# Another share of the taps of a 31-tap convolution for GpSimd, with its products formed on ScalarE, and the attention mask loaded a stage earlier

## The chip, the cores and the metric

The kernel runs on one core of a Trainium2 chip. The metric is the device time of one execution in microseconds, here as the median of several runs; one more execution was recorded by the hardware profiler, and every row below is from that one. PE is TensorE (its weight loads are PEld), DVE is VectorE, ACT is ScalarE, POOL is GpSimd and SP is SyncE, which only issues transfers here.

## The reference

The reference is a two-layer diffusion backbone over 1024 latent tokens and 256 context tokens with a model width of 1024. The change is in the token mixer of the first layer, which has two parallel parts: a convolution module on 512 channels and an attention of 8 heads inside a window. Cut to what matters:

```python
def conformer_conv(z, conv_w, conv_b, ln_g, ln_b):
    val, gate = z[..., :512], z[..., 512:]
    u = val * jax.nn.sigmoid(gate)
    u = dwconv(u, conv_w, conv_b, 15, 15)        # 31 taps, each channel by itself
    return jax.nn.silu(layer_norm(u, ln_g, ln_b))

def mixer_ab(hl, hc, w_in, ...):
    glu, q, k, v = split(h @ w_in)               # for latent and context tokens
    a = conformer_conv(glu, ...)
    b = window_gqa_latent(rope(q), q, rope(k), v, k_ctx, v_ctx, sink)
    return concat(a, b) @ w_out

# inside the attention, for blocks of 128 queries:
s_lat = where(abs(qpos - kpos) <= 128, q @ k.T * scale, -1e30)
p_lat, p_ctx, _ = joint_softmax([s_lat, s_ctx, sink])
```

## The kernel before

The tokens lie in the free dimension and the channels on the 128 partitions. They come in three groups of 512, 512 and 256 (`TOK`). Every projection is done with weights and activations split into a high and a low part, three matmuls for each slice of 128 input channels (lines 316 to 318). `wcol` loads a block of 128 output columns on SP's queue (line 291), ScalarE rounds it to the high part `wh` (line 296), and line 299 subtracts to get the low part `wl`, on VectorE or GpSimd as the letters of `WS` for the stage say in turn.

`proj0` is the stage of the projections of layer 0. Its steps stand in `PROJ0`: `glu(i)` makes the gated input U of one of four blocks of 128 convolution channels, from two weight blocks; `qproj` and `kvproj` make q, k and v. `gemm` takes PSUM from a pool of four banks (`mm`). After each `gemm`, `pump` advances background generators by a time that it is credited with: the convolutions (`conv`), the modulation vectors (`mods`), and the stacking of the queries (`qstack`).

`conv(i, U)` does one block of channels. The accumulator A lies in the three PSUM banks of the pool `ca`, of which there is one. ScalarE starts it with the middle tap (line 642). Of the other 30 taps, VectorE adds 22 into A, one instruction of 1295 columns each (line 654). The first 8 (`PTAPS`) go to GpSimd: one instruction forms a product P (line 649) in one of two buffers `cp`, and another adds it to the one before (line 651). Line 657 adds both sums on VectorE into `co`, from where three transfers on SP's queue (line 659) store it to HBM. The layer norm reads it from there in the course of the attention.

`mods(0, 1..3, None, pa)` runs in the background of this stage with its tiles in the stage's pool. Its matmul results leave PSUM through line 346, on ScalarE.

`attn0` follows. It closes `ca`, opens the two double banks `big` for the scores in its place, and opens the SBUF pool `m0b` where `m0a`, the pool of `proj0`, has been. Its first act is to load the mask `msk` (1152 columns) and the sinks on ScalarE's queue (lines 805 and 807). For each pair of heads and block of queries, `scores` computes scores into `big` (lines 865 and 872), adds the mask and takes the maximum on VectorE (line 877), exponentiates on ScalarE (line 882) and divides; `pv` transposes and multiplies by v. 40 such steps are chained, three of them ahead of their `pv`.

The order of the instructions on each engine is fixed at build time by a planner. It goes by the order of the program and by its own estimate of when an instruction can start, so a later instruction may be put ahead of an earlier one on the same engine. On the chip each engine then works through its list in order. A tile that lies where an earlier tile has been waits until that one's readers have ended, transfers too.

Of the kernel before, what the change touches and what calls it, by code (L numbers as in the profile page):

```python
# [11 lines left out]
F32 = mybir.dt.float32  # L12
F32R = mybir.dt.float32r
AF = mybir.ActivationFunctionType
ALU = mybir.AluOpType
# [5 lines left out]
SEQ = 1024  # L21
CTX = 256
# [3 lines left out]
TOK = (512, 512, 256)  # L26
# [6 lines left out]
LAGC = 2  # L33
GRPS = 3, 3, 3, 3, 3, 3, 1, 3
SQB = 3
P0W = "V"
YR = 6.0
YP = 18.0
YL = 1.5, 1.0, 1.5
# [2 lines left out]
YF = 6.0  # L42
O0 = "G"
MS = ((0, 5), (1, 1), (1, 0), (1, 2), (1, 4), (1, 3), (1, 5)), ()
PTAPS = 8
WS = {"p0": P0W, "o0": O0, "f0": "GV", "c0": "GV", "p1": "GV", "m1": "G", "o1": "V", "f1": "G"}
PB0 = 4
LAG0 = 3
# [51 lines left out]
def tile_backbone(ctx: ExitStack, tc: tile.TileContext, a: dict, out: bass.AP):  # L100
    nc = tc.nc
    V, S, G, T = nc.vector, nc.scalar, nc.gpsimd, nc.tensor
# [21 lines left out]
    def nm(s):  # L124
        uid[0] += 1
        return f"{s}{uid[0]}"
# [17 lines left out]
    def page(shape, dt=F32, s="pg"):  # L144
        return pgp.tile(shape, dt, tag="pg", name=nm(s))
# [59 lines left out]
    def tmp(n=512, dt=F32):  # L205
        return tp.tile([128, 512], dt, tag="t512", name=nm("t"), bufs=4)[:, 0:n]
# [55 lines left out]
    for r, items in enumerate(rows):  # L262
        n = 0
# [71 lines left out]
    def mods(l, idx, pre=None, pool=None):  # L335
        w = 512 if pre else (256 if pool else 128)

        def load(n, q):
            raw = (pool or wmp[0]).tile([128, 4, w], F32, tag="wm", name=nm("wm"), bufs=2)
            c0 = idx * D + n * w  # L340
            nc.sync.dma_start(raw, a["w_mod"][l, q * 512:q * 512 + 512, c0:c0 + w].rearrange("(k p) m -> p k m", p=128))
            return raw

        def fin(ps, n):
            t = tmp(w)
            (S.copy if pool else V.tensor_copy)(t, ps)
            yield YF
            pr = bank()
            nb = w // 128
            for m in range(nb):  # L350
                T.matmul(pr[:, 2 * m:2 * m + 2], t[:, m * 128:m * 128 + 128], sel, start=True, stop=True)
            mod_fin(l, idx, nb * n, nb, 2, pr)

        if pre:
            pss = [bank(), bank()]
            for q in range(2):
                for n in range(2):
                    for j in range(4):
                        T.matmul(pss[n][32 * j:32 * j + 32], sc[:, q * 4 + j], pre[q * 4 + j][:, n * 512:n * 512 + 512], start=q == 0, stop=q == 1)
            for n in range(2):  # L360
                yield from fin(pss[n], n)
            return
        nn = 1024 // w
        raws = [load(0, 0), load(0, 1)]
        yield 6.0
        for n in range(nn):
            ps = bank()[:, 0:w]
            for q in range(2):
                for j in range(4):
                    T.matmul(ps[32 * j:32 * j + 32], sc[:, q * 4 + j], raws[q][:, j], start=q == 0, stop=q == 1)  # L370
                if n + 1 < nn:
                    raws[q] = load(n + 1, q)
            yield from fin(ps, n)
            yield YM0 if pool else YM
# [235 lines left out]
    CW, UW = SEQ + 15 + CTX, SEQ + 15 + CTX + 30  # L610
    COFF = (0, 512, SEQ + 15)

    def mixer0(hs, nxt, xs0):
        w = a["ab_w_in"][0]
        pc = ph[0]
        rcos, rsin = pc.tile([128, 1024], F32, name="rcos", bufs=1), pc.tile([128, 1024], F32, name="rsin", bufs=1)
        protr = pc.tile([128, 3, 128], F32R, name="protr", bufs=1)
        with tc.tile_pool(name="m0a", bufs=1) as pa:
            prep = proj0(hs, w, pa, rcos, rsin, protr, xs0)
        psum_side("big", 2)  # L620
        cat = Lazy()
        with tc.tile_pool(name="m0b", bufs=1) as pb:
            attn0(pb, *prep, cat)
        ws[0] = "o0"
        with tc.tile_pool(name="m0o", bufs=8 * len(YPO)) as po:
            for i, g in enumerate(GO0):
                if i < 2:
                    spawn(cat.load(GO0[i + 1]), "cat")
                ys, sq, last = outproj(a["ab_w_out"][0], cat, g, (lambda g: [po.tile([128, 512], F32, tag="y", name=nm("y")) for _ in range(8)]) if g in YPO else (lambda g: acts(g, 8, F32, "y")), lambda g: PO0[g], range(7, -1, -1) if g in OR0 else None)
                drain("cat")  # L630
                spawn(update(0, g, ys, sq, 2, last, True, (0, 3, 4) if g < 2 else None, nxt, PU0[g]))
            pumping[0] = True
            while not posted >= {(0, g) for g in YPO}:
                advance(flows["norm"])
            pumping[0] = False

    def proj0(hs, w, pa, rcos, rsin, protr, xs0):
        def conv(i, U):
            wc = lambda k: cols("acw", k * 4 + i)
            A = wide()[:, 0:CW]  # L640
            B = None
            S.activation(A, U[:, 15:15 + CW], AF.Identity, scale=wc(15), bias=cols("acb", i))
            taps = [k for k in range(31) if k != 15]
            pt, dt = taps[:PTAPS], taps[PTAPS:]
            nch = 6
            for c in range(nch):
                for k in pt[c::nch]:
                    P = pa.tile([128, CW], F32, tag="cp", name=nm("cp"), bufs=2)
                    G.tensor_scalar(P, U[:, k:k + CW], wc(k), 1.0, ALU.mult, ALU.mult)
                    if B is not None:  # L650
                        G.tensor_add(P, P, B)
                    B = P
                for k in dt[c::nch]:
                    V.scalar_tensor_tensor(A, U[:, k:k + CW], wc(k), A, ALU.mult, ALU.add)
                yield CY
            O = pa.tile([128, CW], F32, tag="co", name=nm("co"), bufs=2)
            V.tensor_add(O, A, B)
            for g in range(3):
                nc.sync.dma_start(cd[g][:, i], O[:, COFF[g]:COFF[g] + TOK[g]])

        st = pa.tile([128, CW], F32, tag="cp", name=nm("par"), bufs=2)
        for r in range(1, 5):
            spawn(params(r, st[:, r * 128 - 128:r * 128]), "par")

# [29 lines left out]
        def kvproj():  # L694
            prot = tmp(384).rearrange("p (a b) -> p a b", a=3)
            nc.scalar.dma_start(prot, a["rot"])
            V.tensor_copy(protr, prot)
            wk, wv = wcol(w, 1536), wcol(w, 1664)
            for g in range(3):
                n = TOK[g]  # L700
                ps = bank()[:, 0:n]
                gemm(ps, wk, *hs[g])
                if g < 2:
                    kh, kl = tmp(dt=F32R), tmp(dt=F32R)
                    split(ps, kh, kl)
                else:
                    V.tensor_copy(KFC[:, 0], ps)
                p2 = bank()[:, 0:n]
                gemm(p2, wv, *hs[g])
                S.copy(VF[:, OFF[g]:OFF[g] + n] if g < 2 else KFC[:, 1], p2)  # L710
                if g < 2:
                    pp = bank()
                    T.matmul(pp, protr[:, 0], kh, start=True, stop=False)
                    T.matmul(pp, protr[:, 0], kl, start=False, stop=True)
                    dst, m2 = KF[:, OFF[g]:OFF[g] + n], tmp()
                    V.tensor_mul(dst, ps, rcos[:, OFF[g]:OFF[g] + n])
                    V.tensor_mul(m2, pp, rsin[:, OFF[g]:OFF[g] + n])
                    V.tensor_add(dst, dst, m2)
# [81 lines left out]
        drain("bg")  # L800
        return KH[0:2], KH[2], vstack, kstack, qstack, qs

    def attn0(pc, KH, KC, vstack, kstack, qstack, qs, cat):
        msk = pc.tile([128, 1152], F32, name="msk")
        nc.scalar.dma_start(msk, a["win_mask"])
        sink = pc.tile([128, 8], F32, name="sink")
        nc.scalar.dma_start(sink, a["b_sink"].to_broadcast([128, 8]))
        nsink = pc.tile([128, 8], F32, name="nsink")
        V.tensor_scalar_mul(nsink, sink, -1.0)

        cath, catl = [[], [], []], [[], [], []]

# [38 lines left out]
        def scores(i, b, RAW, ROT, res):  # L851
# [6 lines left out]
            for j in range(2):  # L858
                s = bank2()
                if b < 8:  # L860
                    k0, k1 = max(0, b - 1), min(8, b + 2)
                    nw = 128 * (k1 - k0)
                    kt = list(range(k0, k1)) + [8, 9]
                    for x in range(2):
                        T.matmul(s[:, 512 - nw:512], ROT[j][:, b * 128:b * 128 + 128], KH[kv][x][:, k0 * 128:k1 * 128], start=x == 0, stop=x == 1)
                    q = RAW[j][0][:, b * 128:b * 128 + 128]
                    mk = msk[:, 0:640] if 0 < b < 7 else (msk[:, 128:640] if b == 0 else msk[:, 640:1152])
                else:
                    nw, kt, mk = 0, [8, 9], msk[:, 384:640]
                    q = RAW[j][1][:, (b - 8) * 128:(b - 8) * 128 + 128]  # L870
# [960 lines left out]
```

## Time and profile before

| | us |
|---|---|
| median of 3 runs | 3089.76 (3085.82 to 3090.44) |
| the profiled execution, its own time | 3090.51 |
| its span, first to last instruction | 3088.7 |
| PE busy in the span | 2934.9 (95%) |
| DVE busy | 1746.5 (57%) |
| ACT busy | 1093.5 (35%) |
| POOL busy | 991.6 (32%) |

The time outside the span is 1.8 us. PE's busy time counts overlapping matmuls by modelled ends, so what tells is where PE stands idle and at which granted clock it works: 1.00 is 2.4 GHz and 0.50 is 1.2 GHz.

### The profile page before, as it was taken

Reading aid. Unit: us, or ns where it says so; the run is one execution under the profiler, and the core shown is the slowest. Engines: PE = TensorE matmul, PEld = TensorE weight load, DVE = VectorE, ACT = ScalarE, POOL = GpSimd, SP = SyncE. Lnnn points to the kernel's source line nnn. Section 1 sums busy time; section 2 is a strip of 40 time slices with the busy share of each in tenths; the row PEclk is TensorE's granted clock in tenths of the full one; section 3 lists DMA queues with packets and bytes.
Section 4 is the critical chain, followed back from the end, with each engine's and each line's share of the span. In section 5 each row is a group of like instructions: output and inputs, shape, how many; then the busy total and the mean of one; then the engine's idle time right before and its main releaser. Section 6 shows DMA issues by size and latency. Waiting matters only on the chain. (4 is left out here: it accounts for less than half of the span.)

```text
span 3088.7 us, 37477 instructions
## 1 busy us (share of the span) xinstructions
PE 2934.9 (95%) x14441; PEld 2351.5 (76%) x14441; DVE 1746.5 (57%) x2631; ACT 1093.5 (35%) x1631; POOL 991.6 (32%) x730
## 2 busy tenths in 40 slices
PE   6997899899999999999999789999998999999998
PEld 4886777678888888889987556666686888888886
DVE  4799883664654555558645886667355132232234
ACT  4213784532221122145533763333344322111213
POOL 4676445821110011055432351110253222112223
PEclk8998999999999999999999899999999999999999
DMA  8343113434432444269844230010152121111212
GB/s 296 117 132 99 38 34 109 139 104 132 143 128 78 130 140 144 84 195 280 275 148 145 92 112 27 31 39 28 58 160 89 48 62 55 34 44 53 62 41 109
DMA packets 330768, 327.04 MB, mean 106 GB/s; under 512 B 27121, under 2 KB 280734, under 8 KB 330590
## 3 DMA queue, kind: packets, MB, share of 16 engines
q1 hardware_dynamic: 326784, 321.74, 32.5%
q10 hardware_dynamic: 3806, 2.91, 0.3%
q8 instruction: 113, 1.85, 0.2%
q14 instruction: 65, 0.53, 0.1%
HBM read 255.36 MB, written 69.21 MB: 105 GB/s over the span
## 5 line engine op out<-in xcount | busy, mean ns | idle before, releaser
L299 POOL TENSOR_TENSOR wl<-wr,wh 128x1024 fp32r<-128x1024 f32 x154 | 380.7, 2472 | 1302.6 <-ACT wh L296 1253.6
L296 ACT CAST wh<-wr 128x1024 fp32r<-128x1024 f32 x248 | 259.7, 1048 | 1063.1 <-PE big L317 678.8
L316 PE MATMUL big<-hh,wh 128*128 128x512 f32 x1376 | 540.4, 393 | 4.9 <-DVE ga L1489 2.7
L317 PE MATMUL big<-hl,wh 128*128 128x512 f32 x1376 | 537.9, 392 | 3.1 <-POOL hl L504 3.1
L318 PE MATMUL big<-hh,wl 128*128 128x512 f32 x1376 | 537.5, 391 | 0.6 <-DVE wl L299 0.6
L316 PE MATMUL mm<-hh,wh 128*128 128x256 f32 (+1 forms) x1000 | 346.3, 347 | 10.8 <-DVE i L1035 9.5
L317 PE MATMUL mm<-hl,wh 128*128 128x256 f32 (+1 forms) x1000 | 339.0, 339 | 4.5 <-POOL hl L504 2.6
L318 PE MATMUL mm<-hh,wl 128*128 128x256 f32 (+1 forms) x1000 | 337.8, 338 | 3.3 <-POOL wl L299 2.3
L316 PEld LDWEIGHTS big<-hh,wh 128*128 128x128 f32 x1376 | 260.1, 189 | 61.5 <-ACT hh L499 3.4
L317 PEld LDWEIGHTS big<-hl,wh 128*128 128x128 f32 x1376 | 260.1, 189 | 58.7 <-POOL hl L504 4.3
L318 PEld LDWEIGHTS big<-hh,wl 128*128 128x128 f32 x1376 | 259.9, 189 | 55.4 <-DVE wl L299 1.0
L1557 PE MATMUL mm<-zh,wh 128*128 128x512 f32 x704 | 276.6, 393 | 1.2 <-ACT xt L1660 0.7
L1559 PE MATMUL mm<-zh,wl 128*128 128x512 f32 x704 | 275.4, 391 | 0.0
L1558 PE MATMUL mm<-zl,wh 128*128 128x512 f32 x704 | 274.9, 391 | 0.3 <-DVE zl L323 0.3
L1564 DVE TENSOR_TENSOR acc<-acc,mm 128x512 f32<-128x512 f32 x224 | 150.7, 685 | 179.5 <-PE mm L1559 179.2
L474 POOL TENSOR_TENSOR sq<-t,sq 128x512 f32<-128x512 f32 (+1 forms) x153 | 194.6, 1274 | 170.5 <-ACT t L470 153.9
L1489 DVE SCALAR_TENSOR_TENSOR ga<-big,C,ga 128x1023 f32<-128x1023 f32 x86 | 110.2, 1281 | 235.1 <-ACT ga L1502 233.7
L316 PEld LDWEIGHTS mm<-hh,wh 128*128 128x128 f32 x1000 | 192.3, 192 | 37.3 <-DVE i L1035 9.9
L317 PEld LDWEIGHTS mm<-hl,wh 128*128 128x128 f32 x1000 | 192.1, 192 | 30.1 <-POOL hl L504 5.4
L318 PEld LDWEIGHTS mm<-hh,wl 128*128 128x128 f32 x1000 | 191.9, 192 | 24.2 <-POOL wl L299 3.2
L399 DVE SCALAR_TENSOR_TENSOR wa<-wm,sc,wa 128x256 f32<-128x256 f32 x280 | 149.2, 558 | 89.8 <-DMA wm<-in_w_mod_dram 87.5
L299 DVE TENSOR_TENSOR wl<-wr,wh 128x1024 fp32r<-128x1024 f32 x94 | 131.6, 1400 | 108.4 <-ACT wh L296 104.4
(350 smaller groups left out, 5267.7 us busy)
## 6 DMA issues: line engine op xcount, KB each, us to landing
wr<-in_ffn_w_up_dram SPq DMA_DIRECT2D x132, 512.0 KB, 4.9
wm<-in_w_mod_dram SPq DMA_DIRECT2D x224, 128.0 KB, 2.2
wr<-in_ffn_w_down_dram SPq DMA_DIRECT2D x44, 512.0 KB, 3.5
wm<-in_w_mod_dram SPq DMA_DIRECT2D x40, 512.0 KB, 7.4
xd<-x SPq DMA_DIRECT2D x38, 512.0 KB, 4.4
x<-xd SPq DMA_DIRECT2D x38, 512.0 KB, 5.8
wr<-in_ab_w_out_dram SPq DMA_DIRECT2D x24, 512.0 KB, 7.5
wdd<-wh SPq DMA_DIRECT2D x22, 512.0 KB, 2.6
```

What stands on the lines that cost most here:

```text
L296: S.copy(hi[:, 0:nk, 0:m], raw[:, 0:nk, 0:m])
L299: (G if e[wn[0] % len(e)] == "G" else V).tensor_sub(lo[:, 0:nk, 0:m], raw[:, 0:nk, 0:m], f32(hi[:, 0:nk, 0:m]))
L316: T.matmul(ps, wh, xh[k], start=i == 0, stop=False)
L317: T.matmul(ps, wh, xl[k], start=False, stop=False)
L318: T.matmul(ps, wl, xh[k], start=False, stop=i == n - 1)
L399: V.scalar_tensor_tensor(acc[:, v], raw, sc[:, k, v:v + 1], acc[:, v], ALU.mult, ALU.add)
L474: self.eng.tensor_add(self.acc[-1], t, self.acc[-1])
L1489: V.scalar_tensor_tensor(dst[:, lo:hi], src[:, lo + d - o:hi + d - o], k, dst[:, lo:hi], ALU.mult, ALU.add)
L1557: T.matmul(ps, wh, zh, start=j == j0, stop=False)
L1558: T.matmul(ps, wh, zl, start=False, stop=False)
L1559: T.matmul(ps, wl, zh, start=False, stop=j == j1 - 1)
L1564: V.tensor_add(ys[g][c], ys[g][c], ps)
```

## The change

GpSimd's part of a convolution grows from 8 taps to 10, and VectorE's shrinks from 22 to 20. The products for GpSimd are formed by ScalarE, in three buffers in place of two, so that GpSimd only adds. The stage's weight splits alternate between GpSimd and VectorE (`P0W`), where all were on VectorE. The results of `mods` leave PSUM on VectorE. The last convolution's result goes to a page of the kernel's common pool (`page`, 24 of 4 KB per partition) and a common temporary tile, as two additions, where it went to the stage's pool as one. Mask and sinks get a place in the mixer's outer pool and are loaded in `kvproj`, on ScalarE's queue; the part of the mask that only the last block needs is loaded as before, in `attn0`.

```diff
-P0W = "V"
+P0W = "VG"
-PTAPS = 8
+PTAPS = 10
 WS = {"p0": P0W, "o0": O0, ...}
...
         def fin(ps, n):
             t = tmp(w)
-            (S.copy if pool else V.tensor_copy)(t, ps)
+            V.tensor_copy(t, ps)
...
         with tc.tile_pool(name="m0a", bufs=1) as pa:
-            prep = proj0(hs, w, pa, rcos, rsin, protr, xs0)
+            masks = [pc.tile([128, n], F32, name=s_, bufs=1) for s_, n in (("msk", 640), ("sink", 8), ("nsink", 8))]
+            prep = proj0(hs, w, pa, rcos, rsin, protr, xs0, masks)
...
                 for k in pt[c::nch]:
-                    P = pa.tile([128, CW], F32, tag="cp", name=nm("cp"), bufs=2)
-                    G.tensor_scalar(P, U[:, k:k + CW], wc(k), 1.0, ALU.mult, ALU.mult)
+                    P = pa.tile([128, CW], F32, tag="cp", name=nm("cp"), bufs=3)
+                    S.mul(P, U[:, k:k + CW], wc(k))
                     if B is not None:
                         G.tensor_add(P, P, B)
                     B = P
...
-            O = pa.tile([128, CW], F32, tag="co", name=nm("co"), bufs=2)
-            V.tensor_add(O, A, B)
+            if i < 3:
+                O = pa.tile([128, CW], F32, tag="co", name=nm("co"), bufs=1)
+                V.tensor_add(O, A, B)
+                parts = [O[:, COFF[g]:COFF[g] + TOK[g]] for g in range(3)]
+            else:
+
+                O, OC = page([128, 1024], F32, "co"), tmp(CTX)
+                V.tensor_add(O, A[:, 0:SEQ], B[:, 0:SEQ])
+                V.tensor_add(OC, A[:, SEQ + 15:CW], B[:, SEQ + 15:CW])
+                parts = [O[:, 0:512], O[:, 512:1024], OC]
             for g in range(3):
-                nc.sync.dma_start(cd[g][:, i], O[:, COFF[g]:COFF[g] + TOK[g]])
+                nc.sync.dma_start(cd[g][:, i], parts[g])
...
         def kvproj():
             prot = tmp(384).rearrange("p (a b) -> p a b", a=3)
             nc.scalar.dma_start(prot, a["rot"])
+            nc.scalar.dma_start(masks[0], a["win_mask"][:, 0:640])
+            nc.scalar.dma_start(masks[1], a["b_sink"].to_broadcast([128, 8]))
+            V.tensor_scalar_mul(masks[2], masks[1], -1.0)
             V.tensor_copy(protr, prot)
...
-        msk = pc.tile([128, 1152], F32, name="msk")
-        nc.scalar.dma_start(msk, a["win_mask"])
-        sink = pc.tile([128, 8], F32, name="sink")
-        nc.scalar.dma_start(sink, a["b_sink"].to_broadcast([128, 8]))
-        nsink = pc.tile([128, 8], F32, name="nsink")
-        V.tensor_scalar_mul(nsink, sink, -1.0)
+        msk, sink, nsink = masks
+        msk7 = pc.tile([128, 512], F32, name="msk7")
+        nc.scalar.dma_start(msk7, a["win_mask"][:, 640:1152])
```

## Rows read from the trace of the kernel before

**Rows 1.** Stretches of 50 us: busy time (instructions) per engine, granted clock, DMA share, GB/s.

```profile
150.00:200.00 50.00, 50.00 (x294) 40.88 (x293) 47.92 (x37) 8.98 (x14) 37.53 (x20) 1.00 0.53 160
300.00:350.00 50.00, 37.47 (x293) 30.59 (x294) 43.46 (x109) 33.76 (x70) 19.74 (x28) 0.79 0.26 80
400.00:450.00 50.00, 48.71 (x446) 38.74 (x444) 41.79 (x115) 42.76 (x91) 29.15 (x40) 1.00 0.01 2
```

**Rows 2.** Waits of PE, 60 to 302 us and 302 to 460 us: total, times, longest.

```profile
PE mm L755 <- POOL sraw L751: 3.0, 1, 3.0
...
PE big L865 <- DVE mx L877: 11.2, 6, 8.9
PE big L865 <- DVE co L657: 7.0, 1, 7.0
```

**Rows 3.** Timeline of the change of stage: start, duration, instruction, idle before.

```profile
295.15 0.44 PE L735 MATMUL mm<-ident,kfc 128*128 128x128 f32 x2 [0.56 <-ACT t L784]
301.06 1.50 DVE L657 TENSOR_TENSOR co<-ca,cp 128x1295 f32<-128x1295 f32 x1
302.58 1.28 SPq L659 DMA_DIRECT2D cd<-co  x3
302.61 0.79 PE L865 MATMUL big<-k,srot 128*128 128x256 f32 x2 [7.03 <-DVE co L657]
307.10 2.84 DVE L751 TENSOR_TENSOR sraw<-qsrc,sraw 64x512 fp32r<-64x512 f32 x4
307.40 0.35 ACTq L805 DMA_DIRECT2D msk<-in_win_mask_dram  x1
312.36 0.98 POOL L220 TENSOR_SCALAR p<-sink 128x2 f32<-128x2 f32 x4 [12.73 <-DMA qsrc<-qd]
312.88 0.68 DVE L877 CUSTOM_DVE_ANT_0 p<-big,msk 128x512 f32<-128x512 f32 x1
313.63 1.01 PE L865 MATMUL big<-k,srot 128*128 128x384 f32 x2 [8.94 <-DVE mx L877]
```

**Rows 4.** Stretches of 10 us around both idle times, columns as in rows 1.

```profile
270.00:280.00 10.00, 6.34 (x24) 4.53 (x23) 9.96 (x5) 0.00 (x0) 9.77 (x5) 0.84 0.32 103
280.00:290.00 10.00, 10.00 (x50) 8.60 (x49) 9.81 (x12) 1.41 (x3) 3.28 (x4) 0.82 0.21 65
310.00:320.00 10.00, 5.83 (x19) 5.46 (x20) 7.85 (x23) 4.52 (x9) 1.68 (x5) 0.50 0.37 118
```

**Rows 5.** DVE's groups, 60 to 302 us: count | busy, mean ns of one | idle before.

```profile
L654 DVE SCALAR_TENSOR_TENSOR ca<-u,C,ca 128x1295 f32<-128x1295 f32 x88 | 138.0, 1568 | 4.7 <-ACT ca L642 2.9
L299 DVE TENSOR_TENSOR wl<-wr,wh 128x1024 fp32r<-128x1024 f32 x11 | 22.5, 2047 | 3.6 <-ACT wh L296 3.6
L657 DVE TENSOR_TENSOR co<-ca,cp 128x1295 f32<-128x1295 f32 x4 | 6.0, 1501 | 0.9 <-POOL cp L651 0.9
L707 DVE COPY kfc<-mm 128x256 f32<-128x256 f32 x1 | 0.4, 408 | 0.0
```

**Rows 6.** POOL's groups, 60 to 302 us.

```profile
L651 POOL TENSOR_TENSOR cp<-cp,cp 128x1295 f32<-128x1295 f32 x28 | 86.8, 3100 | 2.3
L649 POOL TENSOR_SCALAR cp<-u,C 128x1295 f32<-128x1295 f32 x32 | 47.4, 1480 | 39.5 <-DVE co L657 14.6 <-DVE u L687 12.7 <-PE mm L275 9.5
L299 POOL TENSOR_TENSOR wl<-wr,wh 128x1024 fp32r<-128x1024 f32 x3 | 8.0, 2692 | 6.9 <-PE mm L735 6.9
```

**Rows 7.** ACT's groups: the first 60 to 302 us, the second 302.5 to 460 us.

```profile
L642 ACT ACTIVATE ca<-u,C 128x1295 f32<-128x1295 f32 x4 | 5.7, 1434 | 6.0 <-DVE co L657 6.0
...
L224 ACT ACTIVATE p<-p,den 128x640 f32<-128x640 f32 x24 | 19.9, 828 | 2.0 <-DVE den L884 1.6
```

**Rows 8.** Timeline of ACT, POOL and DVE at single places.

```profile
55.34 1.23 DVE L299 TENSOR_TENSOR wl<-wr,wh 128x1024 fp32r<-128x1024 f32 x1
157.65 0.60 ACT L679 ACTIVATE u<-mm 128x512 f32<-128x512 f32 x1 [5.41 <-PE mm L318]
275.30 6.29 POOL L751 TENSOR_TENSOR sraw<-qsrc,sraw 64x512 fp32r<-64x512 f32 x4
```

More of the change, by code (lines that the diff above doesn't have):

```diff
@@ L622, in mixer0 @@
         with tc.tile_pool(name="m0b", bufs=1) as pb:
-            attn0(pb, *prep, cat)
+            attn0(pb, *prep, cat, masks)
         ws[0] = "o0"
@@ L635, in mixer0, with proj0 @@
             pumping[0] = False
-    def proj0(hs, w, pa, rcos, rsin, protr, xs0):
+    def proj0(hs, w, pa, rcos, rsin, protr, xs0, masks):
         def conv(i, U):
@@ L655, in conv @@
                 yield CY
-            O = pa.tile([128, CW], F32, tag="co", name=nm("co"), bufs=2)
-            V.tensor_add(O, A, B)
+            if i < 3:
[7 more added lines that the diff above has]
+                parts = [O[:, 0:512], O[:, 512:1024], OC]
             for g in range(3):
-                nc.sync.dma_start(cd[g][:, i], O[:, COFF[g]:COFF[g] + TOK[g]])
-        st = pa.tile([128, CW], F32, tag="cp", name=nm("par"), bufs=2)
+                nc.sync.dma_start(cd[g][:, i], parts[g])
+        st = pa.tile([128, CW], F32, tag="cp", name=nm("par"), bufs=3)
         for r in range(1, 5):
@@ L801, in proj0, with attn0 @@
         return KH[0:2], KH[2], vstack, kstack, qstack, qs
-    def attn0(pc, KH, KC, vstack, kstack, qstack, qs, cat):
-        msk = pc.tile([128, 1152], F32, name="msk")
-        nc.scalar.dma_start(msk, a["win_mask"])
-        sink = pc.tile([128, 8], F32, name="sink")
-        nc.scalar.dma_start(sink, a["b_sink"].to_broadcast([128, 8]))
-        nsink = pc.tile([128, 8], F32, name="nsink")
-        V.tensor_scalar_mul(nsink, sink, -1.0)
+    def attn0(pc, KH, KC, vstack, kstack, qstack, qs, cat, masks):
+        msk, sink, nsink = masks
+        msk7 = pc.tile([128, 512], F32, name="msk7")
+        nc.scalar.dma_start(msk7, a["win_mask"][:, 640:1152])
         cath, catl = [[], [], []], [[], [], []]
@@ L866, in scores @@
                     q = RAW[j][0][:, b * 128:b * 128 + 128]
-                    mk = msk[:, 0:640] if 0 < b < 7 else (msk[:, 128:640] if b == 0 else msk[:, 640:1152])
+                    mk = msk[:, 0:640] if 0 < b < 7 else (msk[:, 128:640] if b == 0 else msk7)
                 else:
```

## The prediction

> **What bounds the kernel now.** I began with the table of stretches. In the projections PE and VectorE are both full: from 150 to 200 us PE is busy for all 50.00 us at full clock and VectorE for 47.92, while ScalarE works 8.98 and GpSimd 37.53 [rows 1]. In the attention, from 400 to 450, PE is at 48.71, VectorE at 41.79 and ScalarE at 42.76 [rows 1]. Between the two, from 300 to 350, PE has 37.47 and a granted clock of 0.79 [rows 1]: something is lost at the change of stage.
>
> Then I read PE's list of waits, to see for whom. Two entries stand out there: 7.0 us for line 657, the last addition of the last convolution, and 11.2 us for the softmax maxima, 8.9 of them at once [rows 2]. Ahead of them, 3.0 us go to GpSimd's stacking of the queries [rows 2].
>
> The timeline says what the two are. PE's last transposes of the projections end at 295.59. The first scores go into banks that held the accumulator A; line 657 reads A from 301.06 to 302.56, and at 302.61 the scores start [rows 3]. They fill both double banks, and the next scores wait until line 877 has emptied one. That needs the mask. Its transfer waits until the memory of the old stage is free, and the stores of the last result, issued at 302.58, still read there; so it is issued at 307.40, and line 877 begins at 312.88 and PE goes on at 313.63 [rows 3]. Between 302.61 and 309.94 VectorE isn't idle, though: it works off q and k, whose last piece is the row at 307.10 [rows 3]. So the second idle time has two lower ends, the mask's arrival and VectorE's backlog, and only 312.88 - 309.94 = 2.9 us are the mask's alone. That decides how I count below: PE's gaps and VectorE's work are two separate limits, and the smaller gain counts.
>
> **VectorE.** Removed: 2 taps in each of 4 convolutions, 8 x 1.568 = 12.5 us [rows 5]. Splits: the stage has 14 weight blocks, which alternate; the odd ones go to GpSimd, and of these five (5, 7, 9, 11, 13) lie in the full stretch, 5 x 2.047 = 10.2 us [rows 5]. Added: 12 evictions of `mods` at the nearest copy's 0.408, 4.9 us [rows 5]; line 657 as two instructions in the last convolution, for which I take 0.1 (less than one more short copy). The negated sinks now wait for a transfer in `kvproj`; their cost is bounded by nothing below and by 312.36 - 307.40 = 5.0 us above, the time from the mask's issue to the first use of the sinks [rows 3]. I take 1.4, nearer to nothing since the line behind it in the program waits for a transfer issued just before anyway; behind it on VectorE stand the taps of the convolution, and behind them line 657. Sum: -12.5 - 10.2 + 4.9 + 0.1 + 1.4 = -16.3 us.
>
> One subtraction took 1.23 us at 55.34, ahead of the first convolution; the mean in the stage is 2.05 [rows 5, 8]. The Trainium skill, "SBUF — State Buffer", section "Who interferes with whom", has a rule for this: a VectorE instruction with two SBUF inputs and a GpSimd instruction that reads SBUF shut each other out. By that the five splits free only their own 5 x 1.23 = 6.2 us, with the rest returning wherever other such pairs meet, and VectorE's sum would be -12.3. The row measures what they hold of VectorE's time now, so I keep 10.2.
>
> **VectorE's limit.** Its backlog would end at 309.94 - 16.3 = 293.6, and with the mask long there line 877 can start: 312.88 - 293.6 = 19.2 us sooner.
>
> **PE's limit.** Gone if line 657 comes in time: 7.0. Gone if the mask lies ready: 8.9, less what VectorE's limit takes. That is 15.9 [rows 2]. Ahead of it PE waited 3.0 us at 277 for GpSimd's subtraction of the queries, which ran from 275.30 because the convolution's sums were ahead of it [rows 2, 8]; and from 280 to 290 the granted clock was 0.82, so for (1 - 0.82)/0.5 = 36% of 10 us PE worked at 1.2 GHz and lost 1.8 us [rows 4]. If GpSimd is done sooner, these 4.8 go as well: 20.7 us.
>
> **GpSimd.** Removed: 32 products of 1.480, 47.4 us. Added: 8 additions of 3.100, 24.8, and five to seven splits of 2.692, 13.5 to 18.8 [rows 6]. Net -4 to -9 us. With three buffers it also need not stand 14.6 us for line 657 of the convolution before, as its products did [rows 6]. So its chain should end sooner, not later. This costs nothing as long as line 657 waits on VectorE's taps; it waited 0.9 us for GpSimd in all [rows 5].
>
> **ScalarE.** Added: 40 products. The same kind of instruction, SBUF to SBUF with a scale per partition, took 0.828 us for 640 columns; line 642 took 1.434 for 1295 into PSUM [rows 7]. Between 0.83 and 1.43 I take 1.40: 56 us, over some 190 us in which ScalarE works about 9 of 50 [rows 1]. The cover is large. It costs something only through its order: behind a product that waits for a buffer stand the evictions of PSUM (line 679) and the high parts of the weights. A PSUM result comes every 6.01 us, and ScalarE stood idle 5.41 of them before one [rows 8]. With four banks PE can run on for about two results, 12 us, before a late eviction stops it.
>
> **The rest.** The two loads move on ScalarE's queue past the work of `attn0`; as a free place waits for them, they are two issues. The rest of the mask still waits for the old memory at the head of `attn0`, on ScalarE's queue, but for line 657 alone and not for stores, and the last block needs it seven steps later. The page for the last result comes from those that the projections' inputs leave; the last q projection frees enough. If it came late, line 657 would be held until PE's last matmul, some 295, which is where PE's limit stands anyway.
>
> **Sum.** VectorE's limit gives 19.2, PE's 15.9 to 20.7. I take 17.5, as I expect part of the 4.8 us. The profiled execution then takes 3090.51 - 17.5 = 3073.0. The median of the runs is 0.75 us under that execution, so 3072.3, rounded 3072. What follows is bound by PE and no transfer or date there depends on when it starts, so I let all of it shift.
>
> **Rivals.** About 0.2%, 6 us, is what a measurement can tell from no change.
>
> *Only one of the two waits goes (0.15).* Line 657 stays late, because the planner puts the last taps behind the queries again, or the mask's gap stays VectorE's backlog. For it: from 270 to 290 us VectorE is full, 9.96 and 9.81 of 10 [rows 4], and the backlog is real. Against: 16 us of work less. It gives 8.9, so 3081.
>
> *The gain is given back in the attention (0.10).* The waits leave, and ScalarE or VectorE becomes the bound from 295 on; both were at 42 to 43 of 50 there, with PE at 48.7 [rows 1]. The filler that ran in the idle time must find another place. Three quarters of 17.5 given back: 3085.
>
> *GpSimd is late (0.04).* Line 657 needs its sum too. An addition takes it 3.100 against 1.501 on VectorE [rows 5, 6]; 36 additions and five splits are 125 us, against 134 for sums and products before [rows 6], and before it held line 657 up by 0.9 us in all [rows 5]. So it would have to slip through its order, behind ScalarE's products. Each microsecond by which its last sum ends behind VectorE's last tap is one lost, and 15 would give 3087. "GPSIMD Engine Reference" of the Trainium skill, section "Engine selection", says to leave elementwise additions to VectorE, since GpSimd is about twice as slow; the rows agree on the ratio.
>
> *Slower: ScalarE's queue holds PE up (0.07).* A product needs the buffer that the addition two taps earlier frees, so ScalarE can be held to GpSimd's 3.1 us per tap. If the planner, thinking GpSimd faster, puts all products of a convolution ahead of an eviction, the tenth waits for eight additions, 25 us; less PE's 12 us of cover, 13 us are lost. In two convolutions that is 26 - 17.5 = +8.5: 3098. It decides once PE loses 17.5/4 = 4.4 us in each. Against it: each credit of `pump` releases at most two products, and where ScalarE already waits for this chain, at line 642, it lost 6.0 us in three times [rows 7], so the plan is near the clock.
>
> **Numbers.** Main case 0.64, both waits gone, gain 12 to 24. The low end is PE's 20.7 and, from 310 to 320, 5.83 us of work at a clock of 0.50, half of which is 2.9 [rows 4]: 3089.76 - 23.6 = 3066; VectorE's bound without the sinks' wait, 20.6, lies within it; I go 2 lower for rounding, 3064. The high end takes in the single wait (3081) and a part of giving back, 3084. Faster: 0.64 + 0.15 = 0.79. Same: 0.10 + 0.04 = 0.14. Slower: 0.07.
>
> **What would show it.** Right: line 657 of the last convolution ends before PE's last projection does; the first scores follow the transposes within 1 us, the second pair within 3; VectorE has 80 taps and 7 to 8 splits, GpSimd no products; the granted clock from 290 to 310 is near 1. PE's wait for the queries at 277 is gone, or else the gain is nearer 16. Wrong: new waits of PE for line 679 or line 296 between 100 and 280, or waits of the attention's matmuls for softmax that add up to ten or more; or the planner's order of the later stages changes and takes or gives there what this stage doesn't explain.

## The result, and the profile after

The kernel became slower: 3107.55 us median (3104.23 to 3112.61, 4 runs) against 3090.1 us for the kernel before on the same chip, a ratio of 1.0054 (95% interval 1.0043 to 1.0066). The profiled execution took 3108.61 us; its span is 3106.8, 18.1 us more than before.

Where these came in is read from four starts in the timelines: ScalarE's first sigmoid (line 679, now 688), PE's last transposes of the projections (line 735, now 747), and the second pair and the last of the scores (line 865, now 874).

| us | before | after | length before | length after | change |
|---|---|---|---|---|---|
| first sigmoid | 69.64 | 75.74 | 69.6 | 75.7 | +6.1 |
| last transposes | 295.15 | 315.74 | 225.5 | 240.0 | +14.5 |
| second pair of scores | 313.63 | 320.47 | 18.5 | 4.7 | -13.8 |
| last scores | 451.09 | 465.84 | 137.5 | 145.4 | +7.9 |
| end of the span | 3088.7 | 3106.8 | 2637.6 | 2641.0 | +3.4 |

The gain at the change of stage is there, 13.8 us. The loss lies ahead of it, in the start and in the projections, and more than half of the gain went again in the attention. The last row stays unexplained; in the kernels below this length lies between 2633.7 and 2645.6 us with no order that I could see.

**The start.** Timeline of the kernel after: ScalarE's DMA issues, VectorE, PE.

```profile
13.46 0.44 ACTq L706 DMA_DIRECT2D msk<-in_win_mask_dram  x1
15.93 0.36 ACTq L707 DMA_DIRECT2D sink<-in_b_sink_dram  x1
...
21.76 0.17 DVE L708 TENSOR_SCALAR nsink<-sink 128x8 f32<-128x8 f32 x1 [14.64 <-DMA sink<-in_b_sink_dram]
21.84 1.88 DVE L584 COPY x<-mm 128x512 f32<-128x512 f32 x3
...
22.58 1.76 PE L583 MATMUL mm<-ident,xr 128*128 128x128 f32 x7 [4.49 <-DVE x L584]
```

The loads are written in `kvproj`, but their tiles lie where nothing has been before, so nothing holds them back: the planner put them right behind the parameter loads on ScalarE's queue, and the negation fourth in VectorE's list. VectorE stood 14.64 us until the 8 columns of sinks had come, with the evictions of the first transposes (line 584) behind. ScalarE's own first eviction of these came at 16.33, behind the two issues, and at 14.00 before.

**The projections.** The table of stretches, to be held against [rows 1]:

```profile
150.00:200.00 50.00, 47.29 (x278) 38.21 (x277) 42.03 (x37) 20.22 (x20) 30.00 (x14) 1.00 0.40 123
300.00:350.00 50.00, 43.16 (x271) 36.16 (x270) 42.14 (x79) 33.95 (x63) 22.37 (x25) 0.83 0.28 88
```

From 150 to 200 us nothing is full any more: PE is down from 50.00 to 47.29, VectorE from 47.92 to 42.03, GpSimd from 37.53 to 30.00; only ScalarE, with the products, is up from 8.98 to 20.22 and still far from full. So engines must be waiting for each other. The waits of PE and of ScalarE, 60 to 316 us (total, times, longest), say which:

```profile
PE mm L351 <- DVE t L346: 5.6, 2, 4.1
PE mm L316 <- ACT u L688: 4.8, 2, 3.7
PE mm L316 <- ACT vf L722: 3.4, 1, 3.4
...
ACT cp L650 <- POOL cp L652: 47.1, 25, 3.9
```

None of the three waits of PE stands in [rows 2]; together they are 13.8 us. The fourth line is what I took for the cause: 25 of ScalarE's 40 products (line 650) stood waiting for an addition of GpSimd (line 652). One such place in the timeline, ScalarE, GpSimd and PE:

```profile
217.87 1.39 ACT L650 ACTIVATE cp<-u,C 128x1295 f32<-128x1295 f32 x1 [1.42 <-POOL cp L652]
223.14 1.37 ACT L650 ACTIVATE cp<-u,C 128x1295 f32<-128x1295 f32 x1 [3.88 <-POOL cp L652]
224.42 1.06 ACT L688 ACTIVATE u<-mm 128x512 f32<-128x512 f32 x2
...
217.80 2.41 POOL L299 TENSOR_TENSOR wl<-wr,wh 128x1024 fp32r<-128x1024 f32 x1
220.17 9.00 POOL L652 TENSOR_TENSOR cp<-cp,cp 128x1295 f32<-128x1295 f32 x3
...
214.16 0.50 PE L351 MATMUL mm<-sel,t 128*128 128x2 f32 x4
220.29 1.07 PE L370 MATMUL mm<-wm,sc 128*32 128x256 f32 x16
225.05 0.58 PE L316 MATMUL mm<-hh,wh 128*128 128x256 f32 x1 [3.69 <-ACT u L688]
```

PE was through with a result of `glu` at 214.16, where it goes on to line 351. The sigmoid of that result began only at 224.42, behind a product that stood 3.88 us for GpSimd, which had a weight split (line 299) ahead of its addition. PE stopped at 221.36, after line 370, and went on at 225.05.

In this way, over a PSUM bank that is evicted late, PE lost 8.2 of the 13.8 us. The other 5.6, its two waits for line 346, came by way of VectorE. The longer of them, in ScalarE, VectorE and PE:

```profile
131.03 1.38 ACT L650 ACTIVATE cp<-u,C 128x1295 f32<-128x1295 f32 x1 [1.71 <-POOL cp L652]
132.32 1.03 ACT L296 CAST wh<-wr 128x1024 fp32r<-128x1024 f32 x1
...
133.38 1.76 DVE L299 TENSOR_TENSOR wl<-wr,wh 128x1024 fp32r<-128x1024 f32 x1 [7.02 <-ACT wh L296]
136.54 0.41 DVE L346 COPY t<-mm 128x256 f32<-128x256 f32 x1
...
137.00 0.61 PE L351 MATMUL mm<-sel,t 128*128 128x2 f32 x4 [4.09 <-DVE t L346]
```

The high part of a weight (line 296) stood in ScalarE's list behind products, VectorE stood 7.02 us for it, and the eviction of `mods` stood behind that. At the other of the two VectorE had stood 7.20 us for the middle tap (line 643), with which ScalarE starts the accumulator, behind products as well. In all, VectorE waited 15.4 us for line 296 and 13.1 for line 643, where it had been 3.6 and 2.9 [rows 5].

Nor are waits the whole of the 14.5 us. The stretch of the projections, before and after, and 5 us of it right behind the wait of 3.69:

```profile
69.64:295.15 225.51, 218.64 (x1242) 177.03 (x1242) 202.93 (x175) 57.39 (x96) 155.76 (x82) 0.97 0.36 115
75.74:315.74 240.00, 223.02 (x1242) 181.19 (x1242) 187.17 (x181) 105.65 (x124) 143.21 (x64) 0.95 0.33 105
225.00:230.00 5.00, 4.95 (x23) 4.95 (x24) 1.99 (x2) 0.48 (x1) 4.09 (x2) 0.50 0.30 99
```

PE stands idle for 17.0 us in place of 6.9 (the 3.0 for the queries [rows 2] are gone), which makes 10.1. The same 1242 matmuls take 4.4 us longer, and the granted clock is 0.95 on average where it was 0.97: behind the wait of 3.69 us it is 0.50, which is 1.2 GHz.

**The change of stage.** Timeline of VectorE and PE, against [rows 3]:

```profile
308.45 1.22 DVE L664 TENSOR_TENSOR co<-ca,cp 128x1024 f32<-128x1024 f32 x1
315.60 0.41 DVE L665 TENSOR_TENSOR t<-ca,cp 128x256 f32<-128x256 f32 x1
315.74 0.44 PE L747 MATMUL mm<-ident,kfc 128*128 128x128 f32 x2
316.07 0.50 PE L874 MATMUL big<-k,srot 128*128 128x256 f32 x2
318.44 1.24 DVE L739 TENSOR_TENSOR k<-kf,k 64x1024 fp32r<-64x1024 f32 x1
320.47 1.01 PE L874 MATMUL big<-k,srot 128*128 128x384 f32 x2 [3.18 <-DVE mx L886]
```

The scores follow the transposes without a gap, and the wait for the first maximum (line 886) is 3.18 us and no longer 8.94. But VectorE still has pieces of q and k to do (lines 739, 778); from 316 to 475 us PE waits another 4.8 us for line 886, in six pieces, where before it was 2.3 beside the long one [rows 2].

### The profile page after: what moved, and what is told of

Its sections match the earlier page's. It is cut to its first block, busy times and chain, and to the rows that moved or that the text cites. A ratio compares the mean times of both kernels' runs of the same rounds, so it can differ in the third digit from the quotient of the medians.

```text
span 3106.8 us, 37494 instructions
## 1 busy us (share of the span) xinstructions
PE 2951.9 (95%) x14441; PEld 2364.1 (76%) x14441; DVE 1726.1 (56%) x2629; ACT 1142.4 (37%) x1659; POOL 985.5 (32%) x713
## 5 line engine op out<-in xcount | busy, mean ns | idle before, releaser
L299 POOL TENSOR_TENSOR wl<-wr,wh 128x1024 fp32r<-128x1024 f32 x161 | 396.2, 2461 | 1350.6 <-ACT wh L296 1300.6
L299 DVE TENSOR_TENSOR wl<-wr,wh 128x1024 fp32r<-128x1024 f32 x87 | 113.7, 1307 | 119.2 <-ACT wh L296 115.4
```

Of the source, the lines that this page charges most:

```text
L299: (G if e[wn[0] % len(e)] == "G" else V).tensor_sub(lo[:, 0:nk, 0:m], raw[:, 0:nk, 0:m], f32(hi[:, 0:nk, 0:m]))
```

## The experiments

My theory, A: ScalarE's products wait for GpSimd's additions, PSUM evictions stand behind them in ScalarE's list, and PE runs out of banks. The rivals: the 55 us of products are simply too much for ScalarE (F); the additions are too many for GpSimd (K); the evictions of `mods`, now on VectorE, stop PE; the start alone is the loss. For the wait for line 665 that shows up below there are two more: the place of its result (G), or VectorE's backlog of taps (H). "Projections" in the table runs from the first sigmoid to the last transposes, "change" to the second pair of scores, "attention" to the last scores, all in us and from the profiled execution; the ratio is to the kernel before on the same chip. Two of the profiled executions lie off their medians: that of m1 took 3112.79 us, that of c3 3073.66.

| kernel | median | ratio (95%) | first sigmoid | projections | change | attention |
|---|---|---|---|---|---|---|
| before | 3090.1 | 1 | 69.6 | 225.5 | 18.5 | 137.5 |
| after | 3107.55 | 1.0054 (1.0043 to 1.0066) | 75.7 | 240.0 | 4.7 | 145.4 |
| s2_hold | 3100.69 | 1.0030 (1.0018 to 1.0042) | 67.9 | 241.6 | 4.7 | 145.4 |
| m1_mods_act | 3103.95 | 1.0041 (1.0025 to 1.0056) | 78.2 | 237.1 | 4.7 | 145.2 |
| p1_prod_pool8 | 3092.43 | 1.0003 (0.9992 to 1.0015) | 73.9 | 220.4 | 11.6 | 142.2 |
| b1_stage_only | 3086.35 | 0.9978 (0.9969 to 0.9988) | 68.7 | 220.8 | 11.6 | 142.6 |
| e1_half_add | 3080.34 | 0.9961 (0.9946 to 0.9976) | 68.4 | 222.6 | 4.7 | 143.7 |
| c2_hold_pool8 | 3082.12 | 0.9969 (0.9957 to 0.9982) | 68.6 | 219.8 | 11.7 | 142.6 |
| c5_pool10 | 3093.69 | 1.0004 (0.9994 to 1.0013) | 67.0 | 235.0 | 5.9 | 145.3 |
| c4_pool8_ocpage | 3084.4 | 0.9980 (0.9971 to 0.9990) | 67.7 | 221.4 | 10.6 | 144.9 |
| a8_act8 | 3098.97 | 1.0027 (1.0016 to 1.0038) | 67.8 | 238.7 | 11.6 | 142.5 |
| w2_pool8_splits_v | 3089.96 | 0.9996 (0.9987 to 1.0006) | 69.5 | 224.6 | 16.3 | 139.8 |
| c3_pool8_mods | 3081.33 | 0.9969 (0.9958 to 0.9981) | 66.4 | 219.8 | 7.4 | 143.8 |

**The start (s2_hold).** Each of the two loads waits for the first sigmoid of the last convolution block, and the negation stands in `attn0`.

```diff
-            nc.scalar.dma_start(masks[0], a["win_mask"][:, 0:640])
-            nc.scalar.dma_start(masks[1], a["b_sink"].to_broadcast([128, 8]))
-            V.tensor_scalar_mul(masks[2], masks[1], -1.0)
+            gate(nc.scalar.dma_start(masks[0], a["win_mask"][:, 0:640]), held[0])
+            gate(nc.scalar.dma_start(masks[1], a["b_sink"].to_broadcast([128, 8])), held[0])
...
         msk, sink, nsink = masks
+        V.tensor_scalar_mul(nsink, sink, -1.0)
```

> The changed kernel with the loads of mask and sinks held behind the fourth gated input's first eviction on ScalarE, and the negation of the sinks moved to the attention. Theory A (three places: the start loses 7.0 us because VectorE's fourth instruction waits for the sinks until 21.8 us; the projections lose 13.6 us to ScalarE's order; the stage change gains 13.8): the first block of projections is back where it was, 7 us less, 3100.5. Rival B (the late start only fills a wait that comes anyway): 3107.

The first sigmoid comes at 67.9, 7.9 us earlier than after, and the span is 9.2 us shorter; the projections take 241.6 us, about as long as after. The start is one of two losses, and less than half of them. All kernels below but p1 and m1 hold the loads in this way.

**The products back on GpSimd, 8 taps (p1_prod_pool8), everything else as in the change.**

```diff
-PTAPS = 10
+PTAPS = 8
...
-                    S.mul(P, U[:, k:k + CW], wc(k))
+                    G.tensor_scalar(P, U[:, k:k + CW], wc(k), 1.0, ALU.mult, ALU.mult)
```

> The changed kernel with GpSimd's products on GpSimd again and 8 taps, all else as changed. Theory A (evictions of PSUM stand behind products on ScalarE that wait for GpSimd's additions): 13.6 us less, 3094, and PE's waits for lines 688 and 722 vanish. Rival C (the evictions of the modulation results on VectorE hold PE up): no change in them, 3105 to 3108.

The projections lose 19.6 us against after, and PE's waits for lines 688 and 722 are gone, but for 0.6 us that it had before the change too. A wait of 7.4 us for line 665 is back.

**The evictions of `mods` back on ScalarE (m1_mods_act).**

```diff
-            V.tensor_copy(t, ps)
+            (S.copy if pool else V.tensor_copy)(t, ps)
```

> The changed kernel with the modulation results evicted by ScalarE again. Theory A: PE's 5.6 us of waits for line 346 go, but the products still stand ahead on ScalarE: 3102 to 3107. Rival C: the projections get back most of their 13.6 us: 3094 to 3097.

The interval meets that of after, and PE's wait stays with the other engine's name on it, here in the waits of PE:

```profile
PE mm L351 <- ACT t L346: 5.6, 3, 3.0
```

The theory had expected these 5.6 us to go. On ScalarE the evictions stand behind the products themselves; the engine of these evictions isn't the cause.

**Only what concerns the change of stage (b1_stage_only):** 8 taps, products on GpSimd, splits on VectorE and `mods` on ScalarE as before; the early, held loads, three buffers and the separate last result as in the change.

> The kernel before with only the stage change's part: mask and sinks loaded in the projections and held there, the last convolution's result out of the stage's memory, three product buffers. Theory A: no loss at the start and in the projections; of the 13.8 us at the stage change some 8 come back in the attention as in the changed kernel, if VectorE's backlog is their cause: 3076 to 3084. Rival D (line 657 stays late and the first wait stays): 3081 to 3087. Rival E (the backlog of VectorE takes all of it): 3090.

It is faster than before, and it went as rival D had it. The wait for the mask fell from 8.9 to 1.4 us; the first wait, for line 665, stayed at 7.4.

**Shorter additions (e1_half_add),** s2_hold with GpSimd adding 640 of 1295 columns; the sums of the others are left out:

```diff
-                        G.tensor_add(P, P, B)
+                        G.tensor_add(P[:, 0:640], P[:, 0:640], B[:, 0:640])
```

> The kernel of s2_hold with each of GpSimd's additions over 640 of the 1295 columns only: the sums of the other columns are left out, so its output is not the reference's. ScalarE's products stay as they are, 40 of 1.38 us, but the additions that they wait for take about half. Theory A (an eviction waits because the product ahead of it waits for GpSimd): the projections get back most of their 13.6 us, 3086 to 3091. Rival F (ScalarE's own 55 us of products ahead of the evictions are the cause): stays near s2_hold, 3098 to 3102.

ScalarE's 40 products are all still there, and an addition takes 1.59 us, close to a product. ScalarE's wait for it and what is left of PE's:

```profile
ACT cp L650 <- POOL cp L652: 16.2, 16, 1.7
...
PE mm L351 <- DVE t L346: 2.9, 1, 2.9
```

The waits of line 316 for lines 690 and 725 (688 and 722 in the change) are gone, the projections are 19.0 us shorter than in s2_hold, and the time falls by 20 us to 3080.34, more than the theory had expected (3086 to 3091). That settles it against F: ScalarE has the time for the products; what it hadn't was the wait for GpSimd.

**The best of the parts (c2_hold_pool8):** p1 with the loads held.

> p1_prod_pool8 with the loads held as in s2_hold. If the prices of the start and of the products add: 3092.4 less 7 to 9, 3083 to 3086. If the start's loss is covered when the products are gone: 3092.

**The same with 10 taps (c5_pool10).**

> The kernel of s2_hold (10 taps for GpSimd) with the products on GpSimd in place of ScalarE, nothing else. Theory A: PE's waits for ScalarE's evictions vanish; GpSimd then has 40 x 1.48 + 36 x 3.10 = 171 us of sums and products and 13 to 19 of splits, so its last sum may come late: 3085 to 3093. If the engine of the products doesn't matter: 3100.

c2 beats both kernels; c5 is level with before. Both lie within 1 us of the ranges expected. With 10 taps and its own products GpSimd is full, 48.36 of 50 us, and the shortage moves to the transfers: SP's queue waits 96.4 us for GpSimd's splits, which still read the weight buffers (73.7 in c2), and PE for the weights of the modulation. First the table of stretches of c5, then its waits of PE and SP:

```profile
150.00:200.00 50.00, 45.69 (x243) 35.57 (x244) 39.81 (x32) 5.99 (x8) 48.36 (x29) 0.90 0.51 150
```

```profile
PE mm L370 <- DMA wm<-in_w_mod_dram: 11.5, 4, 9.1
...
SPq L291 <- POOL wl L299: 96.4, 7, 27.9
```

That the one wait hands on to the other is argued from these lines, not tried.

**A place of its own for the context part of the last result (c4_pool8_ocpage),** on c2:

```diff
-                O, OC = page([128, 1024], F32, "co"), tmp(CTX)
+                O, OC = page([128, 1024], F32, "co"), page([128, 1024], F32, "co")[:, 0:CTX]
```

> c2_hold_pool8 with the context part of the last result in a page of its own in place of a common temporary tile. In b1_stage_only PE waited 7.4 us for the second of the two last additions, which stood behind the rotation of the queries. Theory G (it stands there because its temporary tile is taken): PE's wait shrinks to 3 us or less, 3078 to 3082. Rival H (VectorE's backlog of taps sets it): no change against c2_hold_pool8.

PE's wait for line 665 is 7.7 us in both, so G falls. In the timeline of c2's VectorE the last addition follows the last taps with no idle time between, only the rotation of the queries (lines 773 to 775) and the first of the two additions; PE's last transposes had begun at 288.40:

```profile
286.81 6.39 DVE L655 SCALAR_TENSOR_TENSOR ca<-u,C,ca 128x1295 f32<-128x1295 f32 x4
293.11 0.68 DVE L773 TENSOR_TENSOR t<-qsrc,rcos 128x512 f32<-128x512 f32 x1
...
296.12 0.41 DVE L665 TENSOR_TENSOR t<-ca,cp 128x256 f32<-128x256 f32 x1
```

**ScalarE's products with 8 taps (a8_act8),** s2_hold with `PTAPS = 8`; beside c2 only the engine of the products differs.

> The changed kernel with the loads held (no early mask) and 8 taps in place of 10 for GpSimd, its products still formed by ScalarE. The loads-held kernel with 10 such taps took 3100.7 us, the one with 8 taps whose products GpSimd forms 3082.1. Theory A (a product of ScalarE waits for GpSimd's addition, and PSUM evictions stand behind it): the way of waiting is the same with 8 taps, only shorter by two additions of 3.0 us in each convolution, so PE's waits for the sigmoid, the k and v results and the modulation's results remain, some 5 to 10 us in all, and the time lies at 3090 to 3097. Rival K (it is the amount, 10 taps, that overloads GpSimd; with 8 the chain of products and additions keeps pace): no such waits, and since ScalarE's products relieve GpSimd, 3080 to 3084.

The projections take 238.7 us against 219.8 in c2, 18.9 for the engine of the products alone, and two taps less save 2.9 of s2_hold's 241.6. ScalarE's wait and PE's, then the stretch of the projections in a8 and in c2:

```profile
ACT cp L650 <- POOL cp L652: 43.8, 18, 3.1
...
PE mm L351 <- DVE t L346: 5.3, 2, 4.3
PE mm L316 <- ACT vf L725: 4.3, 1, 4.3
PE mm L316 <- ACT t L799: 2.8, 1, 2.8
```

```profile
67.79:306.49 238.70, 223.00 (x1243) 180.36 (x1242) 194.35 (x183) 94.51 (x116) 117.80 (x55) 0.95 0.35 111
68.56:288.40 219.84, 215.75 (x1242) 175.16 (x1241) 194.65 (x183) 53.70 (x85) 164.49 (x87) 0.98 0.38 119
```

Of the 18.9 us, 11.6 are idle time of PE (15.7 for 4.1) and 7.3 come from the same work at a lower granted clock, 0.95 for 0.98.

K falls, and A's own figure, 3090 to 3097, was too low as well: it is the form of the chain, a product on one engine and its addition on the other, and not its length. More than three buffers for the products, or the splits taken out of GpSimd's list with the products on ScalarE, were not tried.

**All splits on VectorE (w2_pool8_splits_v),** c2 with `P0W = "V"`.

> The kernel with held loads and 8 taps whose products GpSimd forms (3082.1 us), with all weight splits of the stage on VectorE as in the kernel before. The prediction counted five splits as 10.2 us of VectorE's time in the full stretch. If that is what they hold, VectorE's last addition comes up to 10 us later and the time is 3088 to 3092; if, as the rule on shared reading has it, they free only 6.2 us, 3086 to 3089; if VectorE has slack for them, 3082 to 3084.

VectorE's groups, c2 first, then w2, and w2's timeline:

```profile
L655 DVE SCALAR_TENSOR_TENSOR ca<-u,C,ca 128x1295 f32<-128x1295 f32 x88 | 137.9, 1567 | 6.0 <-ACT ca L643 4.4
L299 DVE TENSOR_TENSOR wl<-wr,wh 128x1024 fp32r<-128x1024 f32 x6 | 11.0, 1837 | 3.4 <-ACT wh L296 3.4
```

```profile
L655 DVE SCALAR_TENSOR_TENSOR ca<-u,C,ca 128x1295 f32<-128x1295 f32 x88 | 137.9, 1567 | 1.5
L299 DVE TENSOR_TENSOR wl<-wr,wh 128x1024 fp32r<-128x1024 f32 x11 | 25.0, 2273 | 5.2 <-ACT wh L296 5.2
```

```profile
307.87 0.41 DVE L665 TENSOR_TENSOR t<-ca,cp 128x256 f32<-128x256 f32 x1
```

Five splits more hold 14.0 us more of VectorE, and the last addition comes at 307.87 and not at 296.12, 11.8 us later.

**The evictions of `mods` on ScalarE, in c2 (c3_pool8_mods).**

> The kernel with held loads and 8 taps whose products GpSimd forms (3082.1 us), with the results of the modulation back on ScalarE. If VectorE's backlog of taps sets when the last result of the convolution comes (PE's wait for it was 7.7 us there), 12 evictions of about 0.41 us less on VectorE give up to 4.9 us: 3077 to 3080. If the evictions lie in gaps of VectorE, or ScalarE takes them late, nothing: 3081 to 3084, and the wait stays at 7 to 8.

The wait for line 665 falls from 7.7 to 4.3 us, but the medians, 3081.33 and 3082.12, can't be told apart.

## Why the prediction was wrong, step by step

The forecast was 3072 us, between 3064 and 3084; the kernel took 3107.55. The change of stage gave 13.8 us, and the start took 6.1, the projections 14.5, the attention 7.9 and the rest of the kernel 3.4.

**The failed step: "It costs something only through its order ... about two results, 12 us".** It cost the projections 14.5 us. The mechanism was named as the slower rival, with the right chain in it, and given 0.07; the sign set for it, new waits of PE for line 679 between 100 and 280, is there (line 688, 4.8 us in two). Its form was another: not all products of a convolution ahead of an eviction but at most three in a row, and five waits of PE over the whole stage. Four things in the estimate were off. The cover isn't two results: after the one that was through at 214.16 the next banks went to line 351, to one more result of `glu`, and to line 370, so PE stopped at 221.36, after 7.2 us, for the fifth. The argument against, that line 642 lost only 6.0 us while waiting for the chain [rows 7], came from a place that ScalarE passes four times; a product waits at 25 places, 47.1 us in all. The high parts of the weights were named but not priced: 5.6 of the 13.8 us came over VectorE, which stood for line 296 or 643. And a wait was priced at its length: the granted clock behind the waits, 4.4 us in the projections, was in no term. The point from which it decides, 4.4 us in each convolution, was nearly met by PE's waits (13.8/4 = 3.5), and the start and the attention did the rest. e1_half_add and a8_act8 show the cause from both sides: with additions as short as a product the loss goes though all 40 products stay, and with 8 taps it stays as long as ScalarE forms the products.

**The second failed step: "as a free place waits for them, they are two issues", and 1.4 us for the negated sinks.** The place was free from the first instruction on. The planner doesn't follow the position in the program that I priced, and the bound of 5.0 us was made for a wait in `kvproj`. s2_hold gives 7.9 us at the first sigmoid for the pair of loads and their negation; which of them had what share wasn't tried.

**The change of stage** came as forecast, 13.8 us against 15.9, and by the forecast's mechanism, VectorE's sum: with 20 taps on VectorE the first scores follow the transposes, with long projections (after, s2) and with short ones (e1), or 1.6 us behind them (c5); with 22 they wait 7.4 to 7.7 us for line 665, whoever forms GpSimd's products (p1, b1, c2, a8). The wait moves with VectorE's work: 13.9 us with five splits more (w2), 4.3 with the evictions of `mods` taken off (c3). That is H, and for 22 taps the rival of the single wait (0.15) is how it goes.

**Giving back in the attention** (0.10) was also true, in every kernel: the attention takes 142 to 145 us where the change of stage is short, 139.8 in w2 where it is 16.3, and 137.5 before. The two lengths together are 156.0 us before, 150.1 after and 154.3 in c2. So 13.8 us at the change of stage are worth 5.9. To let all of the gain shift to the end was the third error, 7.9 us. The stretch of the attention, before and after:

```profile
313.63:451.09 137.46, 132.18 (x1160) 106.56 (x1161) 118.72 (x322) 117.24 (x251) 71.50 (x99) 0.97 0.08 25
320.47:465.84 145.37, 136.67 (x1161) 108.24 (x1161) 125.50 (x332) 120.99 (x258) 74.15 (x100) 0.95 0.10 31
```

VectorE has 6.8 us more to do in it, of which 6.1 are pieces of q and k (lines 739, 763, 778) that were done by then before. Of PE's 7.9 us 3.4 are idle time (8.7 for 5.3) and 4.5 the same work at a lower granted clock, 0.95 for 0.97. That PE's added idle time is VectorE's work is argued from its waits for line 886 and wasn't tried.

**VectorE's sum.** The taps gave 12.6 us (138.0 to 125.4) for 12.5, and the evictions of `mods` 5.0 for 4.9. The splits were undersized: 22.5 to 7.9 us here and 14.0 in w2, for 10.2. VectorE, POOL and ACT in the groups of the kernel after, 60 to 316 us, against [rows 5 to 7]:

```profile
L655 DVE SCALAR_TENSOR_TENSOR ca<-u,C,ca 128x1295 f32<-128x1295 f32 x80 | 125.4, 1567 | 14.5 <-ACT ca L643 13.1
L299 DVE TENSOR_TENSOR wl<-wr,wh 128x1024 fp32r<-128x1024 f32 x6 | 7.9, 1313 | 15.4 <-ACT wh L296 15.4
L346 DVE COPY t<-mm 128x256 f32<-128x256 f32 x12 | 5.0, 416 | 0.5 <-PE mm L370 0.5
...
L652 POOL TENSOR_TENSOR cp<-cp,cp 128x1295 f32<-128x1295 f32 x36 | 109.7, 3047 | 29.7 <-ACT cp L650 27.4 <-POOL cp L652 0.2
...
L650 ACT ACTIVATE cp<-u,C 128x1295 f32<-128x1295 f32 x40 | 54.6, 1375 | 51.2 <-POOL cp L652 47.1 <-DVE u L696 4.1
```

**The rule on shared reading.** I had drawn from the Trainium skill, "SBUF — State Buffer", section "Who interferes with whom", that freed splits would give only 6.2 us, as the rest would return at other pairs. It didn't return at the taps: 88 of them take 137.9 us in c2 and in w2. The section itself exempts VectorE instructions with one SBUF input, and the taps have their accumulator in PSUM. So for the taps the trace agrees with the rule, and my use of it was wrong; taking the row's 2.047 us in the sum was the better choice, if still too low.

**Products and GpSimd.** 40 products took 54.6 us for 56, 1.375 each for 1.40. GpSimd lost 47.4 us of products and gained 22.9 of additions and 11.2 of splits, net -13.3 where I had -4 to -9, and yet it stood 27.4 us waiting for ScalarE's products, while ScalarE stood 47.1 for its additions. Each was priced by its own busy time; the chain has both.

**What the corrected sum gives.** The plan without the start and with additions that keep pace with the products is e1_half_add, 3080.34 us against 3091.2 for the kernel before on its chip: some 11 us of gain and not 17.5. It leaves out half of the additions' columns, so it is an estimate of the plan and no kernel to use; c2_hold_pool8 gives 9 us with all of them.

## What to carry to other kernels

Before work moves to an idle engine, ask what that engine makes for others: an instruction that waits there for a slower engine holds all of it that stands behind, PSUM results and also operands that a third engine waits for, and the cover is counted in banks, with every user of the pool, not in idle time. When a load is moved into memory that is free from the start, look for what will hold it back; a planner that starts what it can may put it, and the instruction that needs it, ahead of the first stage. A wait of PE costs more than its length where the granted clock is low behind it: here 10.1 us more of idle time came with 4.4 us of slower matmuls. And a stall at a change of stage isn't worth its length: work that is done in it comes later, and here 13.8 us gave 5.9.

## What was not expected of the hardware

The load of 8 columns for all partitions was issued at 15.93, and the instruction that waited for it began at 21.76, 5.8 us later, behind the mask's transfer on the same queue and among the loads of inputs and weights; which of them held it wasn't tried. And one split of 128x1024 on VectorE has no fixed price: 1.31 us on average after the change (7.9 us for six), 1.84 in c2 and 2.27 in w2, where GpSimd formed products as well. What sets it wasn't tried.
